# The samples' attention as a stream of its own in two weaves of a decoder step

## The chip, the cores and the metric

The kernel runs on one core of a Trainium2 chip, written in Python on a tile layer that allocates buffers from pools, sets all semaphores, and puts each engine's instructions into a fixed order when the program is built. The metric is the device time of one execution in microseconds, the median over runs. Engines are named as in the profile: PE (TensorE: matmuls), DVE (VectorE), ACT (ScalarE), POOL (GpSimd), SP (SyncE, which issues most transfers).

## The reference

One step of a two-layer decoder for a prompt of 1024 tokens and for eight samples of one token each, with the same weights (d = 1024, four heads of 128 in each attention, feed-forward width 2816). Layer 0 has a gated recurrence (HGRN2) beside attention into 256 memory tokens, layer 1 has stick-breaking attention beside the same kind of memory attention; a SwiGLU feed-forward follows each. What the change touches is the attention of the samples:

```
mem_attend(q, mk, mv):       s = q.k * dh**-0.5;  p = softmax(s);  o = p.v
stick_breaking(q, k, v, b):  z = q.k * dh**-0.5 + b
                             tail = sum over later keys of log_sigmoid(-z)
                             w = exp(log_sigmoid(z) + tail);  o = w.v
```

Each sample has 256 memory keys and values of its own in each layer, and in layer 1 two pages of 128 shared keys and values out of a paged pool (`cache_sb_k`, `cache_sb_v`, by `page_table`).

## The kernel before, in words

The prompt is worked in two groups of 512 tokens; group 1 also carries the eight samples as columns 512 to 519 of every activation tile. Activations stand with features on partitions. Every projection (`proj`, L256) streams 128x512 weights in: SP loads a raw piece of four 128x128 blocks (L245, pool of 5 buffers), ACT makes its rounded high half (L250), DVE its low half (L251), and PE runs three matmuls for each block: high weight with high and low input, low weight with high input (L264). Group 0 has one matmul of 512 columns each, group 1 two of 260. A projection's sum stands in one of two accumulators (`mm`), each emptied by ACT or DVE before it is used again: L281 and L474 in the gate and up half of the feed-forward, L403 in the down half.

The feed-forward (`ffn.part`, L464) is cut into five parts of 5, 5, 4, 4 and 4 blocks of the width; a part runs a gate and an up projection of 24 pieces for each block and then eight down projections of 15 or 12 pieces.

Stick-breaking for the prompt (`sb_prompt`, L1042) goes by head and by 128 keys: scores (L1058), bias and softplus on ACT and DVE, tail sums by matmuls with triangles (L1073) into a bank held for the whole head, weights by exp (L1081), value sums (L1085) into another bank held as long. So it holds two banks of the pool `s` (three banks), and the scores rotate through what is left. `mem_attn` (L621) goes by head and by pairs of 128 tokens: scores (L632), maximum (L637), exp (L643), normalised (L649), transposed (L656), value sums (L663).

For the samples, `sample_scores` (L671) copies each sample's query row out to all 128 partitions by a transfer from a scratch in memory (L689, on SP), multiplies the sample's keys with it (L690, DVE, 128x1024) and reduces by head (L691, DVE). `sample_pv` (L696) multiplies the values by the weights (L702, DVE), adds the two halves (L703, DVE), and sums over partitions by a matmul with a one-hot column block (L704, PE), all eight samples into one bank. Keys and values of the memory come by SP (L719), pages by an indirect transfer on POOL (L731); both go through the pool `c` of four buffers, which the prompt's memory attention uses for its own keys and values too.

The bank `ns` is a pool of one, used by `rstd_from` (L288) to sum squares over partitions for the norms, and for transposes in other stages.

All these are generators. `weave` (L222) takes streams with weights, and always steps the stream that is least far along by its weight; what it interleaves is the program's order, which the tile layer takes as the priority when it fixes each engine's order. The two weaves concerned are at L1172 (group 1's merge and memory attention of layer 0 beside group 0's feed-forward parts 2 and 3) and L1198 and L1199 (group 1's attention of layer 1 beside group 0's parts 0 to 3). After the first the last feed-forward part is drained, after the second the out projection (`o1.mm`) of group 1 begins, which reads what all attentions left in `xo`.

Of the kernel before, what the change touches and what calls it, by code (L numbers as in the profile page):

```python
# [22 lines left out]
def tile_decoder(  # L23
# [44 lines left out]
    def nm(s):  # L68
        uid[0] += 1
        return f"{s}_{uid[0]}"  # L70
# [4 lines left out]
    def B(dt=F32):  # L75
        return bpool.tile([P, 512], dt, tag="b", name=nm("b"))
# [4 lines left out]
    def NS():  # L81
        return nsp.tile([P, 512], F32, tag="ns", name=nm("ns"))
# [21 lines left out]
    def S():  # L104
        return smp.tile([P, 512], F32, tag="s", name=nm("s"))
# [107 lines left out]
    def drain(*gens):  # L213
        for g_ in gens:
            for _ in g_:
                pass

    def chain(*gens):
        for g_ in gens:
            yield from g_  # L220

    def weave(*streams):  # L222

        live = [[0, n, g_] for g_, n in streams]
        while live:
            cur = min(live, key=lambda e: e[0] / e[1])
            cur[0] += 1
            try:
                next(cur[2])
            except StopIteration:  # L230
                live.remove(cur)
# [38 lines left out]
    def split_to(dst, src):  # L270
        nc.scalar.copy(dst[0], src)  # L271
        nc.vector.tensor_sub(dst[1], src, dst[0].bitcast(F32))  # L272
# [421 lines left out]
            yield  # L694

    def sample_pv(pT, load, xo, k0):  # L696
        po = S()
        pv4 = pT.rearrange("p (k h b) -> p k h b", k=2, h=H)
        for b in range(NB):
            vt = load(b)  # L700
            v4 = vt.rearrange("p k (h d) -> p k h d", h=H)
            nc.vector.tensor_mul(v4, v4, pv4[:, :, :, b].unsqueeze(3).to_broadcast([P, 2, H, P]))  # L702
            nc.vector.tensor_add(vt[:, 0, :], vt[:, 0, :], vt[:, 1, :])  # L703
            nc.tensor.matmul(po[:NB, :], sel[:, b, :], vt[:, 0, :], start=(b == 0), stop=(b == NB - 1))  # L704
            yield
        ot = B()
        nc.vector.tensor_copy(ot[:NB, :], po[:NB, :])
        pr = S()
        for h in range(H):
            nc.tensor.transpose(pr[:, h * NB : (h + 1) * NB], ot[:NB, h * P : (h + 1) * P], ident[:NB, :NB])  # L710
        for h in range(H):
            d = xo[k0 + h]
            split_to((d[:, 0, G : G + NB], d[:, 1, G : G + NB]), pr[:, h * NB : (h + 1) * NB])
        yield
# [24 lines left out]
    def mem_attn_sample(l, qm, xo):  # L739
        HB = H * NB  # L740
        sc = small([P, 2 * HB], tag="sc", bufs=2)
        yield from sample_scores(qm, mem_loader(cache_mem_k, l), sc)
        pr = S()
        for blk in range(2):
            nc.tensor.transpose(pr[:HB, blk * P : (blk + 1) * P], sc[:, blk * HB : (blk + 1) * HB], ident)
        nmx = small([P, 2], tag="nmx")
        nc.vector.tensor_reduce(nmx[:HB, 0:1], pr[:HB, :NM], axis=AX.X, op=ALU.max, negate=True)
        sm = small([P, 2], tag="sme")
        pe = B()
        nc.scalar.activation(pe[:HB, :NM], pr[:HB, :NM], AF.Exp, bias=nmx[:HB, 0:1], accum_out=sm[:HB, 0:1])  # L750
        nc.vector.reciprocal(sm[:HB, 0:1], sm[:HB, 0:1])
        nc.vector.tensor_scalar(pe[:HB, :NM], pe[:HB, :NM], sm[:HB, 0:1], None, op0=ALU.mult)
        pb = S()
        for blk in range(2):
            nc.tensor.transpose(pb[:, blk * HB : (blk + 1) * HB], pe[:HB, blk * P : (blk + 1) * P], ident[:HB, :HB])
        pT = small([P, 2 * HB], tag="ss")
        nc.vector.tensor_copy(pT, pb[:, : 2 * HB])
        yield
        yield from sample_pv(pT, mem_loader(cache_mem_v, l), xo, H)
# [330 lines left out]
    def sb_sample(Qs, xo):  # L1090
        HB = H * NB
        zb = small([P, 2 * HB], tag="sc", bufs=2)
        yield from sample_scores(Qs, page_loader(cache_sb_k), zb)
        nc.vector.tensor_add(zb, zb, biass.rearrange("p k h b -> p (k h b)"))
        e = small([P, 2 * HB], tag="ss")
        softplus_sp(zb, e, 2 * HB)
        cu = S()
        nc.tensor.matmul(cu[:, 0:HB], trif, e[:, 0:HB], start=True, stop=False)
        nc.tensor.matmul(cu[:, 0:HB], ones, e[:, HB : 2 * HB], start=False, stop=True)
        nc.tensor.matmul(cu[:, HB : 2 * HB], trif, e[:, HB : 2 * HB], start=True, stop=True)  # L1100
        nc.vector.tensor_sub(zb, zb, cu[:, : 2 * HB])
        nc.scalar.activation(zb, zb, AF.Exp)
        yield
        yield from sample_pv(zb, page_loader(cache_sb_v), xo, 0)
# [57 lines left out]
    a1 = mixer_a(1, x1)  # L1162
# [5 lines left out]
    f0 = ffn(0, 0, o0.x)  # L1168
    weave((a1.core(), 22), (f0.part(0), 9))
    a1.open()  # L1170
    weave((a1.sample(), 6), (a1.gate(), 4), (f0.part(1), 9))
    weave((chain(a1.merge(), a1.mem_sample(), a1.mem()), 32), (chain(f0.part(2), f0.part(3)), 16))  # L1172
    drain(f0.part(4))
    xk0, xb0 = [], []
    o1 = out_proj(1, 0, M)
# [18 lines left out]
    b1 = mixer_b(1, xb1)  # L1194
    weave((b1.heads(), 8), (o0.finish(), 17))
    b1.open()
    f0 = ffn(0, 1, o0.x)
    weave((chain(b1.sb(), b1.mem()), 40), (chain(f0.part(0), f0.part(1)), 18))  # L1198
    weave((chain(b1.sb_sample(), b1.mem_sample()), 40), (chain(f0.part(2), f0.part(3)), 16))  # L1199
    o1 = out_proj(1, 1, A, True)  # L1200
    drain(o1.mm(b1.xo))
    weave((o1.finish(), 17), (f0.part(4), 8))
# [35 lines left out]
```

## Time and profile before

| | |
|---|---|
| median of 3 runs | 2554.57 us (2554.53 to 2558.19) |
| the profiled execution | 2554.25 us |
| its span in the profile | 2552.5 us |
| granted TensorE clock, mean | 0.995 |
| DMA queue "hardware_dynamic" | 286.92 MB, 37.3% of the engines' span |
| DMA queue "software_dynamic" | 8.39 MB, 1.1% |

The span leaves out 1.75 us around the program. Busy shares are unions of the instructions' times; matmuls are pipelined, and their ends are modelled. "PEclk" is the share of the full TensorE clock that was granted.

### The profile page before, as it was taken

The page shows a single profiled execution, that of the slowest core. Times are in us where ns is not written, and L with a number is a line of the kernel's source. Part 1 is how long each engine was busy: PE and PEld are TensorE (multiplying, and loading weights), DVE is VectorE, ACT ScalarE, POOL GpSimd, SP SyncE. Part 2 cuts the span into 40 slices and gives each one's busy share as a digit, 9 for nine tenths or more (in the row PEclk, how much of TensorE's full clock was granted, in tenths as well). Part 3 has the DMA queues.
Part 4 walks back from the last instruction along what each step waited for, and adds up shares of the span by engine and source line. Part 5 has one row for each costly group of instructions (what it writes and reads, how often), then busy time and mean ns, then how long its engine had stood idle before and what let it go on. Part 6 is the DMA issues. An engine that isn't in the chain of part 4 may idle for free.

```text
span 2552.5 us, 40535 instructions
## 1 busy us (share of the span) xinstructions
PE 2519.7 (99%) x15653; PEld 2194.2 (86%) x15653; DVE 1557.1 (61%) x2714; ACT 1183.8 (46%) x2187; POOL 41.3 (2%) x59
## 2 busy tenths in 40 slices
PE   8999999999999999999999999999999999999998
PEld 6888898878867888999999989767776798999998
DVE  6666566655675577555544577666678758444445
ACT  6346543243434445555433455566543245443334
POOL 1000000000000000000000000000021000000000
PEclk9999999999999999999999999999999999999999
DMA  6352242233552455322333445322156544323332
GB/s 185 109 162 71 73 151 76 66 112 117 172 179 83 132 156 172 102 85 60 99 92 93 127 151 181 110 85 71 53 175 212 154 125 128 108 87 101 94 92 67
DMA packets 457708, 297.91 MB, mean 117 GB/s; under 512 B 17573, under 2 KB 422642, under 8 KB 457514
## 3 DMA queue, kind: packets, MB, share of 16 engines
q1 hardware_dynamic: 454954, 286.92, 37.3%
q0 software_dynamic: 2560, 8.39, 1.1%
q8 instruction: 123, 2.02, 0.3%
q14 instruction: 71, 0.58, 0.1%
HBM read 265.44 MB, written 29.80 MB: 116 GB/s over the span
## 4 chain that ended last, share of the span: by engine, by line
issue 26%; PE 22%; POOL 1%; DVE 1%; DMA 0%; ACT 0%; POOLq 0%; DVEq 0%
PE mm L264 22%; POOL c L731 1%; PE s L704 0%; DVE c L690 0%; DMA c<-in_cache_sb_v,pidx 0%; DVE sc L691 0%; PE s L1135 0%; PE ns L293 0%; PE s L440 0%; DVE yT L542 0%; PE s L508 0%; DVE yT L539 0%; DVE ws L251 0%; POOLq L1234 0%; DVE t L474 0%
## 5 line engine op out<-in xcount | busy, mean ns | idle before, releaser
L264 PE MATMUL mm<-x,ws 128*128 128x260 f32 (+1 forms) x10080 | 1668.6, 323 | 7.8 <-DVE t L474 3.2
L264 PEld LDWEIGHTS mm<-x,ws 128*128 128x128 f32 x10080 | 1446.1, 189 | 170.0 <-issue 28.3
L250 ACT CAST ws<-w 128x512 fp32r<-128x512 f32 (+1 forms) x800 | 475.6, 595 | 910.4 <-PE mm L264 819.4
L251 DVE TENSOR_TENSOR ws<-w,ws 128x512 fp32r<-128x512 f32 (+1 forms) x800 | 522.4, 658 | 330.9 <-ACT ws L250 323.0
L264 PE MATMUL mm<-m,ws 128*128 128x260 f32 (+1 forms) x3168 | 543.0, 325 | 1.6 <-DVE t L474 0.9
L264 PEld LDWEIGHTS mm<-m,ws 128*128 128x128 f32 x3168 | 453.4, 188 | 60.3 <-issue 15.8
L403 DVE TENSOR_TENSOR r<-r,mm 128x520 f32<-128x520 f32 (+1 forms) x128 | 88.3, 690 | 89.0 <-PE mm L264 88.0
L281 DVE TENSOR_SCALAR t<-mm 128x512 f32<-128x512 f32 (+1 forms) x104 | 72.2, 694 | 108.2 <-PE mm L264 107.1
L474 DVE TENSOR_TENSOR t<-t,mm 128x512 f32<-128x512 f32 (+1 forms) x88 | 60.8, 691 | 116.1 <-PE mm L264 115.9
L285 DVE TENSOR_TENSOR t<-t,t 128x512 f32<-128x512 f32 (+1 forms) x88 | 61.2, 695 | 87.6 <-ACT t L284 87.5
L304 DVE TENSOR_TENSOR st<-st,n 128x512 f32<-128x512 f32 (+1 forms) x98 | 67.1, 691 | 6.9 <-ACT n L303 5.0
L272 DVE TENSOR_TENSOR m<-t,m 128x512 fp32r<-128x512 f32 (+1 forms) x88 | 61.0, 693 | 3.5 <-ACT m L271 1.6
L271 ACT CAST m<-t 128x512 fp32r<-128x512 f32 (+1 forms) x88 | 54.8, 623 | 15.7 <-DVE t L474 8.7
L282 ACT ACTIVATE t<-t 128x512 f32<-128x512 f32 (+1 forms) x88 | 55.8, 635 | 13.1 <-DVE t L281 5.7
L283 ACT ACTIVATE t<-t 128x512 f32<-128x512 f32 (+1 forms) x88 | 55.9, 635 | 2.6
L284 ACT ACTIVATE t<-t 128x512 f32<-128x512 f32 (+1 forms) x88 | 55.9, 635 | 2.3
L902 PEld LDWEIGHTS s<-a,a 128*128 128x128 f32 x448 | 53.4, 192 | 1.2
L902 PE MATMUL s<-a,a 128*128 128x64 f32 x448 | 53.1, 271 | 0.0
L731 POOL DMA_INDIRECT c<-in_cache_sb_k,pidx x16 | 16.6, 1037 | 1868.7 <-DVE r L403 1240.2
L1037 DVE SCALAR_TENSOR_TENSOR b<-b,b 128x512 f32<-128x512 f32 (+3 forms) x48 | 26.8, 558 | 29.6 <-ACT b L1036 29.2
L643 ACT ACTIVATE b<-s,nmx 128x256 f32<-128x256 f32 x64 | 29.8, 470 | 28.7 <-DVE nmx L637 28.7
L1085 PE MATMUL s<-b,a 128*128 128x512 f32 (+3 forms) x96 | 41.5, 514 | 0.3
(298 smaller groups left out, 1945.2 us busy)
## 6 DMA issues: line engine op xcount, KB each, us to landing
w<-in_w_gu SPq DMA_DIRECT2D x352, 256.0 KB
w<-in_w_down SPq DMA_DIRECT2D x160, 256.0 KB
w<-in_w_in_a SPq DMA_DIRECT2D x80, 256.0 KB
w<-in_w_o SPq DMA_DIRECT2D x64, 256.0 KB
w<-in_w_mem_kv SPq DMA_DIRECT2D x32, 256.0 KB
c<-in_cache_mem_k SPq DMA_DIRECT2D x16, 512.0 KB
c<-in_cache_mem_v SPq DMA_DIRECT2D x16, 512.0 KB
w<-in_w_kv SPq DMA_DIRECT2D x32, 256.0 KB
```

Source lines behind the costliest of these rows:

```text
L250: nc.scalar.copy(ws[:, 0, :n, :], raw[:, :n, :])
L251: nc.vector.tensor_sub(ws[:, 1, :n, :], raw[:, :n, :], ws[:, 0, :n, :].bitcast(F32))
L264: nc.tensor.matmul(ps[:, a, : PW[g]], wt, xt[k][:, xi, o : o + PW[g]], start=(k == 0 and wi == 0), stop=(k == nk - 1 and wi == 2),)
L272: nc.vector.tensor_sub(dst[1], src, dst[0].bitcast(F32))
L281: nc.vector.tensor_scalar(sv(x, g), pv(ps, g), -44.0, None, op0=ALU.max)
L283: nc.scalar.activation(d, d, AF.Ln, bias=1.0)
L284: nc.scalar.activation(d, d, AF.Exp, scale=-1.0)
L285: nc.vector.tensor_mul(d, d, x[:, :n])
L304: nc.vector.tensor_add(acc[:, :n], acc[:, :n], t[:, :n])
L403: nc.vector.tensor_add(dst, dst, pv(ps, g))
L474: nc.vector.tensor_mul(sv(sg, g), sv(sg, g), pv(pu, g))
L902: nc.tensor.matmul(plv[:, hh, c, :], K_[:, hh, cs], rhs, start=True, stop=True)
```

## The change

Three edits. The bank for the samples' value sums comes from `ns` in place of `s`. In the first layer's weave the samples' memory attention is no longer a piece of the chain between the merge and the prompt's memory attention, but a stream of its own beside both. In the second layer, two weaves one after the other (the prompt's attentions with feed-forward parts 0 and 1, then the samples' with parts 2 and 3) become one weave of three streams: the prompt's attentions, the samples' attentions, and the four parts. Lines behind the second weave move on by two.

```diff
     def sample_pv(pT, load, xo, k0):
-        po = S()
+        po = NS()
...
-    weave((chain(a1.merge(), a1.mem_sample(), a1.mem()), 32), (chain(f0.part(2), f0.part(3)), 16))
+    weave((chain(a1.merge(), a1.mem()), 12), (a1.mem_sample(), 20), (chain(f0.part(2), f0.part(3)), 16))
     drain(f0.part(4))
...
     f0 = ffn(0, 1, o0.x)
-    weave((chain(b1.sb(), b1.mem()), 40), (chain(f0.part(0), f0.part(1)), 18))
-    weave((chain(b1.sb_sample(), b1.mem_sample()), 40), (chain(f0.part(2), f0.part(3)), 16))
+    weave(
+        (chain(b1.sb(), b1.mem()), 40), (chain(b1.sb_sample(), b1.mem_sample()), 39),
+        (chain(f0.part(0), f0.part(1), f0.part(2), f0.part(3)), 34),
+    )
     o1 = out_proj(1, 1, A, True)
```

## The prediction

> **What bounds the kernel now.** I read the page first, then the busy time by stretch, then what TensorE waited for, and last the order in time around the longest of these waits.
>
> ```profile
> span 2552.5 us, 40535 instructions
> ...
> PE 2519.7 (99%) x15653; PEld 2194.2 (86%) x15653; DVE 1557.1 (61%) x2714; ACT 1183.8 (46%) x2187; POOL 41.3 (2%) x59
> ```
>
> TensorE carries the span, and the change neither adds nor takes away a matmul. Only what TensorE loses between matmuls can be won: idle time, and time at a lower clock. Which of it lies in the two changed stretches, the stretches show:
>
> ```profile
> core 0: us, PE busy (x) PEld busy (x) DVE busy (x) ACT busy (x) POOL busy (x), PEclk, DMA share, GB/s
> 1600.00:1870.00 270.00, 269.20 (x1131) 194.85 (x1130) 171.43 (x326) 163.57 (x328) 0.00 (x0) 1.00 0.27 79
> 1870.00:2030.00 160.00, 152.50 (x619) 110.39 (x618) 129.05 (x180) 51.30 (x95) 29.17 (x28) 0.97 0.65 200
> 675.00:750.00 75.00, 72.20 (x294) 52.02 (x293) 63.25 (x84) 24.55 (x41) 0.00 (x0) 1.00 0.67 203
> 1897.25:1904.07 6.82, 5.29 (x13) 4.13 (x13) 5.61 (x8) 0.56 (x1) 2.87 (x3) 0.50 0.79 243
> 1979.17:1982.58 3.41, 3.41 (x9) 2.64 (x9) 3.41 (x5) 0.00 (x0) 0.00 (x0) 0.50 0.87 240
> 559.22:562.63 3.41, 3.41 (x15) 1.61 (x12) 0.07 (x1) 0.00 (x0) 0.00 (x0) 0.50 1.11 327
> ```
>
> From 1600 to 1870 us the prompt's stick-breaking and memory attention run beside feed-forward parts 0 and 1: TensorE is idle for 270 - 269.20 = 0.8 us. From 1870 to 2030 us the samples' two attentions run beside parts 2 and 3: idle for 7.5 us, and VectorE is busy for 129.05 of 160 us (81%, against 63% before). The fourth and fifth rows are two pieces of that stretch in which the clock stood at half. The busy 5.29 + 3.41 us there would have taken half as long, so the half clock cost 4.35 us. From 675 to 750 us, in the first layer, the samples' attention costs 2.8 us of idle time at full clock.
>
> Who ended the idle time, from 1600 to 2030 us and then from 660 to 870 us:
>
> ```profile
> PE mm L264 <- DVE t L474: 3.2, 2, 1.8
> PE mm L264 <- DVE ws L251: 3.1, 2, 1.5
> PE s L704 <- DVE c L703: 1.2, 2, 1.0
> PE s L1073 <- ACT b L271: 0.4, 2, 0.3
> ```
>
> ```profile
> PE mm L264 <- DVE t L474: 0.9, 1, 0.9
> PE s L704 <- DVE c L703: 0.9, 1, 0.9
> ```
>
> It is VectorE nearly every time, and not with work of long duration: L474 empties a projection's bank, L251 makes the low half of a weight. They are late since they stand behind the samples' work in VectorE's queue. VectorE, then TensorE, around the first long wait:
>
> ```profile
> 1892.91 1.22 DVE L690 TENSOR_TENSOR c<-c,b 128x1024 f32<-128x1024 f32 x1 [1.60 <-issue]
> 1894.05 0.69 DVE L285 TENSOR_TENSOR t<-t,t 128x512 f32<-128x512 f32 x1
> 1894.65 1.21 DVE L691 TENSOR_REDUCE sc<-c 128x8 f32<-128x1024 f32 x1
> 1895.78 0.68 DVE L474 TENSOR_TENSOR t<-t,mm 128x512 f32<-128x512 f32 x1
> 1896.37 1.21 DVE L691 TENSOR_REDUCE sc<-c 128x8 f32<-128x1024 f32 x1
> 1897.50 0.68 DVE L272 TENSOR_TENSOR m<-t,m 128x512 fp32r<-128x512 f32 x1
> 1898.10 1.89 DVE L251 TENSOR_TENSOR ws<-w,ws 128x512 fp32r<-128x512 f32 x3
> ```
>
> ```profile
> 1896.60 0.70 PE L264 MATMUL mm<-x,ws 128*128 128x512 f32 x2 [1.81 <-DVE t L474]
> 1898.84 5.43 PE L264 MATMUL mm<-x,ws 128*128 128x512 f32 x12 [1.53 <-DVE ws L251]
> ...
> 1976.71 0.70 PE L264 MATMUL mm<-x,ws 128*128 128x512 f32 x2 [1.39 <-DVE t L474]
> 1978.95 4.38 PE L264 MATMUL mm<-x,ws 128*128 128x512 f32 x11 [1.54 <-DVE ws L251]
> ```
>
> Two samples' products and sums come in a row, the first held up for 1.60 us; L474 and the weights run after them, and TensorE stands for 1.81 and 1.53 us. From 1976 us the same happens again.
>
> **The change part by part.** *The later weave.* The samples' stream of 39 steps now lies beside all of the prompt's 40 and the 34 of the feed-forward. Instructions and transfers are the same in number; their order is not, on any engine. In the order in which the built programs' instructions stand, only two regions differ: this one, and the first layer's. On VectorE the samples' operations had stood in runs of up to four, with one other instruction or two between runs; now one product and one sum stand in each stretch of ten to sixteen instructions, and two or three together only where two values meet. On TensorE the prompt's chains keep their distance: as many matmuls of other work stand between a score and its tail sum as before.
>
> ```profile
> L691 DVE TENSOR_REDUCE sc<-c 128x8 f32<-128x1024 f32 x16 | 19.3, 1213 | 0.0
> L690 DVE TENSOR_TENSOR c<-c,b 128x1024 f32<-128x1024 f32 x16 | 19.1, 1221 | 1.6 <-issue 1.6
> L703 DVE TENSOR_TENSOR c<-c 128x512 f32<-128x512 f32 x16 | 10.7, 687 | 0.0
> L702 DVE TENSOR_TENSOR c<-c,sc 128x1024 f32<-128x1024 f32 x8 | 9.7, 1220 | 3.7 <-DMA c<-in_cache_sb_v,pidx 3.4 <-issue 0.3
> L702 DVE TENSOR_TENSOR c<-c,ss 128x1024 f32<-128x1024 f32 x8 | 9.6, 1221 | 0.3 <-DMA c<-in_cache_mem_v 0.2
> ```
>
> These 64 operations are 68.4 us of VectorE. All its work in the 430 us is 171.43 + 129.05 = 300.5 us: 70% everywhere in place of 63% and then 81%. A key step is 1.22 + 1.21 = 2.4 us, a value step 1.9 us. What covers one such step is a projection: TensorE has two accumulators, and works on the other while one is emptied. The shortest projections of these parts have 12 matmuls (15 in part 0), the gate and up ones 24:
>
> ```profile
> 1953.09 5.47 PE mm L264 x24
> ```
>
> So 0.228 us each, and covers of 2.7, 3.4 and 5.5 us, plus what the prompt's matmuls in between give. One step fits under each; two and a wait, as at 1892, do not. So I expect the 7.5 us of idle time and the 4.35 us of half clock that followed it to go: **-11.85 us**.
>
> What comes in its place: (1) The calm stretch's idle time, stretched: 0.8 us in 270 is 1.3 in 430, **+0.5**. (2) The query rows. Each of the 16 key steps needs one copied out to all partitions, and SP's queue has these copies among the weight loads, which wait for VectorE to free a raw buffer. From 1870 to 2030 us, and the copies with the first key step that used one:
>
> ```profile
> SPq L245 <- DVE ws L251: 71.0, 36, 13.3
> ```
>
> ```profile
> 1878.31 3.84 SPq L689 DMA_DIRECT2D b<-qd  x7
> ```
>
> ```profile
> 1882.10 1.23 DVE L690 TENSOR_TENSOR c<-c,b 128x1024 f32<-128x1024 f32 x1
> ```
>
> From issue to use are at most 3.8 us. In the new order five of the 16 copies have only 1.6 to 2.6 us of VectorE work between the release of the buffer ahead of them and their key step; at 70% load that is 2.3 to 3.7 us. VectorE then stands for 0.1 to 1.5 us, with an accumulator's evacuation behind it; two of the value loads stand alike. TensorE feels only what exceeds the cover. From nothing to seven times 1.5 = 10.5 us; I take **+1.5**, near the lower end, since seven copies in a row delayed VectorE by only 1.60 us above. (3) More turns between streams: the order has 956 changes into or out of L264 in place of 908, so 24 more interruptions. A matmul that waits for a signal took 0.05 us more than its like that seldom does:
>
> ```profile
> L1073 PE MATMUL s<-b,trir 128*128 128x512 f32 x40 | 18.1, 458 | 0.1
> L1073 PE MATMUL s<-b,cmpr 128*128 128x512 f32 x32 | 10.5, 408 | 0.0
> ```
>
> 24 x 0.05 = **+1.2**, from 0 to twice that (both sides of each may wait). (4) The end: the last prompt head's value product now stands inside the out projection's first piece, some 1.5 us of matmuls ahead of the piece that reads it. Its evacuation is two operations of 0.6 to 0.7 us, so nearly covered: 0, at most 1 us.
>
> *The first layer's weave.* The samples' memory attention starts at once beside the merge and the prompt's memory attention. Its 2.8 us of idle time could go. But in the new order the seventh and eighth query rows stand behind six weight loads, and both key steps, 4.9 us, come while TensorE runs projections of 12 matmuls with a cover of 2.7 us. I leave it at **0**, from -2.8 to +3.2 (a wait as at 1896, 1.81 + 1.53, over what goes).
>
> *The bank.* The value sums sit in the norm sums' bank for eight steps. Nobody else asks for it within either weave (the next norm sum comes after the out projection), so nothing waits: 0. It costs no less by itself, but the weave needs it: stick-breaking holds two of the three other banks, and a sum held in the third would leave none for the scores.
>
> Sum: -11.85 + 0.5 + 1.5 + 1.2 + 0 = -8.65 us. The profiled execution took 2554.25 us, so 2545.6; the median shown, 2554.57, lies 0.3 higher, and my forecast for it is **2545.9 us**. About 0.2% (5.1 us) is what a measurement of this kernel can tell from no change.
>
> **A rule against the trace.** The half clock began at 1897.25 us after idle pieces of at most 1.81 us. The Trainium skill ("TensorE: Matmul & The Clock Gate", Part 1: The HAM clock gate) has the clock fall after at least one idle window of about 3.4 us. No idle time here is so long, so by that rule these 4.35 us are not owed to the stalls, and the sum would be -4.3 us. The trace speaks against it in two places of three, where the half clock starts inside a stall or right after one; the third is the rival below.
>
> **The rivals.**
> - *The half clock is not the stalls'.* The last row of the stretches shows half clock from 559.22 us with TensorE busy for the whole 3.41 us, after thin matmuls (eight rows or columns). The samples' value sums, 128x8, are thin too. If it is they, the half clock stays, wherever they stand: 2545.9 + 4.35 = 2550.3 us. Against it: the same sums from 675 to 750 us left the clock at 1.00.
> - *The stalls only move.* VectorE's sum is unchanged, and some sample steps still meet an evacuation. If half of the 11.85 us stays: 2545.9 + 5.9 = 2551.8 us. For it: the late query rows. Against it: 63% load left 0.8 us idle in 270, and 70% is nearer to that than to 81%.
> - *Slower: query rows block VectorE.* It runs its queue in order; a row held behind weight loads that themselves wait for VectorE stops evacuations and weights together. One event of the kind at 1896 costs 1.81 + 1.53 us idle and 5.29 / 2 at half clock, 6.0 us. Two of them eat the gain up; with four, 2545.9 + 24 = 2570, with three 2563.9 us, the time I give it. It decides once VectorE stands for more than a cover (2.7 to 5.5 us) at a key step. Against it: the longest of VectorE's waits there now is 1.60 us.
>
> **How the numbers follow.** Forecast 0.65, stalls move 0.17, half clock stays 0.06, slower 0.12. The forecast's own range is 2539 (nothing comes in place of the 11.85 us and the first layer's 2.8 goes too) to 2549. For 8 in 10 I reach over the two middle rivals: **2539 to 2553 us**. Faster by over 0.2% (below 2549.5): the forecast and a little of the next, 0.68. Within 0.2%: 0.20. Slower: 0.12.
>
> **What would show it.** Right: in the stretch of some 420 us from the first stick-breaking score to the out projection TensorE idles for 1 to 5 us, the clock stays at 1.00, VectorE's load is level at 70%, and all else keeps its length. Wrong: half-clock pieces at the samples' sums with no idle time (the first rival); waits for L251, L474 or L403 summing to 5 us or more behind L690 (the second and third); a longer stretch without idle time would mean that the turns between streams are dearer than 0.05 us.

## The result, and the profile after

The changed kernel takes 2551.05 us (median of 22 runs, 2548.63 to 2553.59), the kernel before, beside it on the same chips, 2555.13 us (22 runs). The ratio is 0.9984 with a 95% interval of 0.9978 to 0.9991: 4.1 us or 0.16% faster, where 8.65 us were forecast. The profiled execution took 2551.36 us; the head of its page:

```profile
span 2549.6 us, 40536 instructions
...
PE 2518.9 (99%) x15653; PEld 2193.2 (86%) x15653; DVE 1557.2 (61%) x2714; ACT 1186.6 (47%) x2187; POOL 43.8 (2%) x59
```

The engines' work is what it was, and 2.9 us of the span are gone. To see where, I cut the span of each trace at matmuls that every version has: the last one of the samples' recurrence in layer 0 (L853), the first transpose of the first key and value projection (L1014), the first transpose of the samples' keys at the end of the second one (L1027), the next norm sum (L293, after the second weave and its out projection), and the last matmul. Each piece is read from one profiled execution. us:

| kernel | start | first layer's piece | between | second layer's piece | remainder |
|---|---|---|---|---|---|
| before | 609.51 | 323.78 | 620.58 | 528.12 | 464.34 |
| after | 608.66 | 319.93 | 620.40 | 529.94 | 464.35 |

The first layer's weave, entered at nothing in the forecast, gave 3.85 us. The second layer's, for which it was made, gave nothing: 1.8 us longer, which is within the scatter (with the old second weave this piece took 528.1 to 530.2 us in three kernels below). (The expectations below quote these two pieces between slightly different marks, as 311.3 to 307.2 and 474.5 to 476.3; the differences are the same within 0.3 us. All pieces in this part go by the table's marks.)

The busy time by stretch, after: the second weave as a whole, three parts of it, the half clock in it, and the first layer's row of before's list.

```profile
core 0: us, PE busy (x) PEld busy (x) DVE busy (x) ACT busy (x) POOL busy (x), PEclk, DMA share, GB/s
1600.00:2030.00 430.00, 421.22 (x1730) 302.67 (x1729) 300.87 (x506) 216.51 (x421) 27.86 (x24) 0.99 0.41 123
1600.00:1700.00 100.00, 99.03 (x425) 74.45 (x423) 69.12 (x113) 54.29 (x104) 14.45 (x14) 1.00 0.46 139
1700.00:1800.00 100.00, 94.16 (x359) 64.00 (x359) 66.86 (x116) 50.03 (x93) 13.41 (x10) 0.97 0.41 120
1800.00:2030.00 230.00, 228.03 (x950) 164.21 (x949) 164.88 (x280) 112.19 (x225) 0.00 (x0) 1.00 0.40 116
1708.30:1715.13 6.83, 5.51 (x15) 4.47 (x16) 4.79 (x10) 1.44 (x4) 2.24 (x2) 0.50 0.34 83
675.00:750.00 75.00, 75.00 (x325) 57.93 (x325) 51.72 (x81) 30.82 (x61) 0.00 (x0) 1.00 0.47 133
```

VectorE's load is level, 300.87 of 430 us or 70%, as forecast. But TensorE still idles for 8.78 us (8.3 before), 5.84 of them between 1700 and 1800 us, and the half clock there costs 5.51 / 2 = 2.75 us. The last row has no idle time left where before had 2.8 us. Who ended TensorE's idle time from 1600 to 2030 us (total, times, longest):

```profile
PE s L1073 <- DVE b L272: 5.3, 2, 3.7
PE s L1085 <- DVE b L1040: 1.5, 2, 1.3
PE s L1073 <- ACT b L271: 0.9, 2, 0.6
PE s L1073 <- DVE b L1078: 0.2, 1, 0.2
```

Every row of before's list is gone: no L264 waits for L474 or L251 any more. In their place the prompt's own tail sums and value sums (L1073, L1085) wait for VectorE. And VectorE, in the same stretch, waits for transfers:

```profile
DVE c L690 <- DMA b<-qd: 10.7, 9, 4.0
...
DVE c L702 <- DMA c<-in_cache_sb_v,pidx: 3.8, 3, 2.7
...
DVE c L702 <- DMA c<-in_cache_mem_v: 2.1, 3, 1.5
```

The longest such wait in order of time, first in SP's issues, then on VectorE, then on TensorE:

```profile
1700.47 0.55 SPq L689 DMA_DIRECT2D b<-qd  x1
```

```profile
1703.68 0.29 DVE L1040 TENSOR_TENSOR b<-b,sm 128x128 f32<-128x128 f32 x1
1708.00 1.23 DVE L690 TENSOR_TENSOR c<-c,b 128x1024 f32<-128x1024 f32 x1 [4.02 <-DMA b<-qd]
1709.14 0.42 DVE L272 TENSOR_TENSOR b<-b,b 128x256 fp32r<-128x256 f32 x1
```

```profile
1704.86 1.10 PE L264 MATMUL mm<-m,ws 128*128 128x512 f32 x4
1709.62 0.58 PE L1073 MATMUL s<-b,trir 128*128 128x256 f32 x1 [3.66 <-DVE b L272]
1710.00 2.77 PE L264 MATMUL mm<-m,ws 128*128 128x512 f32 x6
```

The query row is issued at 1700.47 and used at 1708.00, 7.5 us later; 1700 to 1708 us is full of other transfers (254 GB/s there, against 123 over the weave). VectorE runs its queue in order and stands at L690 for 4.02 us. Behind it is L272, the low half of a softplus piece, and TensorE, in order too, has L1073 next, which reads it. A second accumulator is no help: the projection's matmuls stand behind L1073.

### The profile page after: what moved, and what is told of

Same layout as the page of the kernel before. It is cut to its first block, busy times and chain, and to the rows that moved or that the text cites. A ratio compares the mean times of both kernels' runs of the same rounds, so it can differ in the third digit from the quotient of the medians.

```text
span 2549.6 us, 40536 instructions
## 1 busy us (share of the span) xinstructions
PE 2518.9 (99%) x15653; PEld 2193.2 (86%) x15653; DVE 1557.2 (61%) x2714; ACT 1186.6 (47%) x2187; POOL 43.8 (2%) x59
## 5 line engine op out<-in xcount | busy, mean ns | idle before, releaser
L264 PE MATMUL mm<-x,ws 128*128 128x260 f32 (+1 forms) x10080 | 1668.4, 323 | 1.4 <-ACT x L355 1.3
L264 PEld LDWEIGHTS mm<-x,ws 128*128 128x128 f32 x10080 | 1443.1, 188 | 166.3 <-issue 29.2
L251 DVE TENSOR_TENSOR ws<-w,ws 128x512 fp32r<-128x512 f32 (+1 forms) x800 | 523.5, 657 | 324.0 <-ACT ws L250 314.6
L264 PE MATMUL mm<-m,ws 128*128 128x260 f32 (+1 forms) x3168 | 544.4, 326 | 0.1
L264 PEld LDWEIGHTS mm<-m,ws 128*128 128x128 f32 x3168 | 455.1, 189 | 53.9 <-issue 7.1
L403 DVE TENSOR_TENSOR r<-r,mm 128x520 f32<-128x520 f32 (+1 forms) x128 | 88.3, 690 | 99.2 <-PE mm L264 97.7
L474 DVE TENSOR_TENSOR t<-t,mm 128x512 f32<-128x512 f32 (+1 forms) x88 | 60.8, 691 | 117.2 <-PE mm L264 117.2
L272 DVE TENSOR_TENSOR m<-t,m 128x512 fp32r<-128x512 f32 (+1 forms) x88 | 61.0, 694 | 3.7 <-ACT m L271 1.6
L1073 PE MATMUL s<-b,trir 128*128 128x512 f32 (+3 forms) x96 | 38.0, 397 | 7.6 <-DVE b L272 5.3
L1085 PE MATMUL s<-b,a 128*128 128x512 f32 (+3 forms) x96 | 41.6, 515 | 1.9 <-DVE b L1040 1.5
```

Source lines behind the costliest of these rows:

```text
L251: nc.vector.tensor_sub(ws[:, 1, :n, :], raw[:, :n, :], ws[:, 0, :n, :].bitcast(F32))
L264: nc.tensor.matmul(ps[:, a, : PW[g]], wt, xt[k][:, xi, o : o + PW[g]], start=(k == 0 and wi == 0), stop=(k == nk - 1 and wi == 2),)
L403: nc.vector.tensor_add(dst, dst, pv(ps, g))
L474: nc.vector.tensor_mul(sv(sg, g), sv(sg, g), pv(pu, g))
```

## The experiments

The first theory: late query rows block VectorE, and that eats the second weave's gain up. The rivals: VectorE's load itself, the bank, SP's queue, or other transfers. "Before" in each result is the kernel before, beside it on the same chip.

**One part of the change at a time.** `e_first` takes the second weave's edit back, `e_second` the first one's, `e_bank` both:

```
e_first, e_bank:
-    weave((chain(b1.sb(), b1.mem()), 40), (chain(b1.sb_sample(), ...), 39), (chain(f0.part(0), ...), 34))
+    weave((chain(b1.sb(), b1.mem()), 40), (chain(f0.part(0), f0.part(1)), 18))
+    weave((chain(b1.sb_sample(), b1.mem_sample()), 40), (chain(f0.part(2), f0.part(3)), 16))
e_second, e_bank:
-    weave((chain(a1.merge(), a1.mem()), 12), (a1.mem_sample(), 20), (chain(f0.part(2), f0.part(3)), 16))
+    weave((chain(a1.merge(), a1.mem_sample(), a1.mem()), 32), (chain(f0.part(2), f0.part(3)), 16))
```

> Only the first layer's weave (and the bank); the second layer as before. In the traces, the piece from the samples' recurrence to the first key and value projection took 311.3 us before and 307.2 after, and the piece with the second layer's weave 474.5 and 476.3. Theory: all of the gain is the first layer's, so this kernel gains 4 us by itself, 0.998 of before, as much as both edits together or more. Rival, as the prediction had it: the second weave carries the gain, and this one is 0 (1.000).

> Only the second layer's weave (and the bank); the first layer as before. Theory: nothing won, since what left the projections' waits came back as waits of the prompt's attention: -1 to +2 us, 1.000 of before. Rival, the prediction: -8.65 us, 0.9966.

> Only the bank of the samples' value sums; both weaves as before. Both theories: nothing, 0 +- 1 us, as the sum has a bank to itself either way. If the bank frees the third score bank for earlier work, up to -1 us.

Measured, against 2553.87 us before (11 runs each): `e_first` 2551.16 us, 0.9991 (0.9982 to 1.0); `e_second` 2554.06, 0.9999 (0.999 to 1.0008); `e_bank` 2553.83, 0.9997 (0.9988 to 1.0006). The first layer's piece is 319.73 us in `e_first`, 323.53 and 323.45 in the two others. The interval of `e_first` just reaches 1, so the times alone don't decide; the pieces do: the gain is the first layer's, the second weave's edit is worth nothing as it stands, and the bank costs nothing that shows.

**No query rows from memory.** `e_noq` leaves out layer 1's query rows and multiplies the sample keys by a tile that is on the chip anyway (in short):

```
-            qb = B()
-            nc.sync.dma_start(qb, qd[b].partition_broadcast(P))
+            qb = row        # layer 1: carry.rearrange("p h k -> p (h k)")
```

> The whole change, but in the second layer the samples' keys are multiplied by a tile that lies ready in the buffers (the recurrent state), not by the query row copied out by a transfer: 16 transfers of 256 KB less, and no wait for them; the samples' outputs are then not theirs. Theory: VectorE's 10.7 us of waits for query rows are what holds up the prompt's chain and idles TensorE, so its idle time in the second weave falls from 8.8 us to 3 us or less and no half clock is left there: 5 to 9 us faster than the change as it is (0.995 to 0.997 of before). Rival: the prompt's chain is held up by VectorE's load of 70% and the one bank left for scores, and the time stays at 0.998.

Measured: 2548.23 us (11 runs), 0.9976 (0.9967 to 0.9985). The second layer's piece falls to 522.94 us, 7.0 less than after, with 4.3 us of idle time from 1600 to 2030 us and no half clock, but the first layer's grows from 319.93 to 325.12. Without the query the products depend on nothing in layer 1, and some run early in the first layer, where they block an accumulator once. TensorE from 700 to 900 us:

```profile
PE mm L264 <- DVE t L474: 3.5, 1, 3.5
```

So this run doesn't settle it: work that left the second weave makes it shorter too. `e_cols` keeps the dependency, and takes the query from the tile of its columns, which hold its features by partition (so the products are not the ones wanted, but as many and as large):

```
+                k4 = kt.rearrange("p k (h d) -> p k h d", h=H)
+                q4 = qc.rearrange("p (h b) -> p h b", h=H)[:, :, b].unsqueeze(1).unsqueeze(3)
+                nc.vector.tensor_mul(k4, k4, q4.to_broadcast([P, 2, H, P]))
```

> The whole change, but in the second layer the samples' keys are multiplied by columns that stand in the buffers from the weave's start on (the query's features by partition) in place of the copied row: no 256 KB copies there, the same count and size of VectorE operations, and they cannot start before the weave; the samples' outputs are then not theirs. It mends the run before it, where the products had run ahead into the first layer: there the second layer's piece was 7.0 us shorter than with the change (529.94 to 522.94 us) and the first layer's 5.2 us longer. Theory: the query rows' waits are what idles TensorE, so the second layer's piece is 5 to 7 us shorter than with the change, the first layer's the same: 0.996 of before. Rival (load of VectorE, one bank for scores): the piece stays near 530 us, 0.998.

Measured: 2549.96 us (11 runs), 0.9989 (0.998 to 0.9998) against 2553.4; the second layer's piece 529.96 us, as in after. **The first theory falls**: without a query row the time is the same. TensorE and VectorE in the same stretch of `e_cols` (L1078 is L1073 of after, L691 the key product, L707 the value product):

```profile
PE s L1078 <- ACT b L271: 4.7, 1, 4.7
```

```profile
DVE c L707 <- DMA c<-in_cache_sb_v,pidx: 5.1, 4, 2.6
...
DVE c L691 <- DMA c<-in_cache_sb_k,pidx: 4.4, 1, 4.4
...
DVE c L691 <- DMA c<-in_cache_mem_k: 1.8, 2, 1.0
...
DVE c L707 <- DMA c<-in_cache_mem_v: 0.5, 2, 0.3
```

The stall has moved to the next transfer: one page of keys holds VectorE until 1608.25 us, for 4.4 us. Behind it on VectorE stands the softplus piece (L1039 there) that ScalarE and then L1078 go by, and TensorE stands for 4.7 us, until 1613.31 us. The new theory: it is not this copy but any load whose product comes to VectorE's head before the data.

**Another queue for the rows.** `e_qact` issues the same copies from ScalarE's queue, so that they don't stand behind weight loads on SP:

```
-            nc.sync.dma_start(qb, qd[b].partition_broadcast(P))
+            nc.scalar.dma_start(qb, qd[b].partition_broadcast(P))
```

> The whole change, with the query rows' copies issued from ACT's queue, not SP's, in both layers: they no longer stand behind weight loads, though their place in time and the transfers beside them are the same. If the rows are late since SP issues them late: waits for rows fall under 3 us, 5 us won, 0.996 of before. If they are late since the transfer itself takes long beside page gathers, weights and keys (issue at 1700.5 us, first use at 1708.0): waits stay near 10 us, and the time at 0.998, or worse, as ACT spends 16 issues more.

Measured: 2550.99 us (11 runs), 0.9991 (0.9982 to 1.0); second layer's piece 528.34. VectorE's waits:

```profile
DVE c L690 <- DMA b<-qd: 8.1, 8, 2.5
...
DVE c L702 <- DMA c<-in_cache_sb_v,pidx: 3.5, 3, 2.5
```

8.1 us in place of 10.7: SP's queue is at most a quarter of it, and the time is the same.

**Products held back until their data can be there.** `e_hold` copies each query row one step ahead, and puts layer 1's key products behind one of two VectorE operations of the other streams, whichever stands last before them in the program: the product in a feed-forward block (L474 of after) or the subtraction from a tail sum (L1078). So they can't be placed much earlier than the weave has them:

```
+    def behind(on):
+        return tc.issue_after(mark[0].ins) if on else nullcontext()
-                nc.vector.tensor_mul(sv(sg, g), sv(sg, g), pv(pu, g))
+                mark[0] = nc.vector.tensor_mul(sv(sg, g), sv(sg, g), pv(pu, g))
...
-                nc.vector.tensor_sub(zb[:, :w], zb[:, :w], rr[:, c0:])
+                mark[0] = nc.vector.tensor_sub(zb[:, :w], zb[:, :w], rr[:, c0:])
...
+            if b + 1 < NB or not late:
+                rows.append(row(b + late))
+            with behind(late):
+                nc.vector.tensor_mul(kt, kt, qb.unsqueeze(1).to_broadcast([P, 2, 512]))
```

`e_holdv` does the same with the value steps:

```
+        ahead = [load(0)] if late else []
...
+            if b + 1 < NB or not late:
+                ahead.append(load(b + late))
+            vt = ahead.pop(0)
+            with behind(late):
+                nc.vector.tensor_mul(v4, v4, pv4[:, :, :, b].unsqueeze(3).to_broadcast([P, 2, H, P]))
```

and `e_vonly` holds the value steps alone.

> The whole change, and in the second layer each query row is copied out one step ahead, while its product is put behind the last VectorE operation of the other two streams that stands before it in the program: 7 to 14 us of VectorE work between the release ahead of the copy and the product, where there were 2 to 7. The same work, the same outputs. Theory: the waits for query rows go (10.7 us to under 2), and with them 5 to 7 us of the second layer's piece: 0.996 of before. Rival one (load): 0.998. Rival two: putting products later fills the end of the weave and moves the stall there, 0.998 or above.

> As the run before, and the value steps likewise: loaded one step ahead, their product put behind the other streams. VectorE waited 2.7 us for one value page with the change. Theory: another 0 to 2 us: 0.995 to 0.996 of before. Rival two (the end of the weave) is stronger here: the last value sum stands later, and the out projection may wait for it, up to 3 us lost.

> Of the run with both kinds of step put behind the other streams (0.9949 of before, 2540.3 us, TensorE idle for 0.5 us of 430) only the value steps; the query rows come as in the change. Theory, as mended by the runs so far: any transfer that VectorE waits for in its queue can stop TensorE, and with one kind taken away the other still does, so the two gains do not add: rows alone gave 2.4 us of the second layer's piece, this one gives 2 to 5 of the 11.7 that both give, 0.996 to 0.998 of before. Rival: the value pages were the whole cause, and this run equals the one with both, 0.995.

`e_hold`: 2549.52 us (11 runs), 0.9987 (0.9978 to 0.9996); second layer's piece 527.55, 2.4 us less than after where 5 to 7 were expected. The rows' waits are gone, those for values have grown (L718; TensorE's L1089 is L1073 of after):

```profile
DVE c L718 <- DMA c<-in_cache_sb_v,pidx: 9.3, 4, 5.0
```

```profile
PE s L1089 <- ACT b L276: 4.3, 1, 4.3
PE s L1089 <- DVE b L277: 2.1, 2, 1.6
```

`e_holdv`: **2540.32 us** (2539.57 to 2542.41, 5 runs) against 2553.4, 0.9949 (0.9936 to 0.9963); second layer's piece 518.21, another 9.3 us less where 0 to 2 were expected. Its stretches, and all that VectorE still waits for transfers:

```profile
1600.00:1870.00 270.00, 269.65 (x1109) 193.05 (x1108) 184.89 (x318) 145.13 (x274) 24.69 (x24) 1.00 0.43 130
1870.00:2030.00 160.00, 159.87 (x710) 117.44 (x709) 116.03 (x196) 75.17 (x155) 0.00 (x0) 1.00 0.38 115
1600.00:2030.00 430.00, 429.52 (x1818) 310.49 (x1817) 300.92 (x513) 220.30 (x429) 24.69 (x24) 1.00 0.41 124
```

```profile
DVE c L722 <- DMA c<-in_cache_mem_v: 0.5, 1, 0.5
```

The same instructions, VectorE with the same 301 us, and TensorE idle for 0.48 us in 430, at full clock. `e_vonly`: 2547.02 us (10 runs), 0.9974 (0.9964 to 0.9983) against 2554.58; piece 522.39, 7.6 us less than after where 2 to 5 were expected, with the rows' waits still there:

```profile
DVE c L706 <- DMA b<-qd: 6.8, 8, 2.7
```

So each half of the hold takes part of it away, and only both take all. From 1600 to 2030 us TensorE's idle time goes with VectorE's waits for transfers, of either kind: 8.78 us idle for 16.6 us of waits in after, 7.20 for 11.1 in `e_hold`, 4.24 for 6.8 in `e_vonly`, 0.48 for 0.5 in `e_holdv`. `e_noq`, which holds nothing back, lies between them as well (4.26 for 6.9). In the weave of three streams the cause is these waits. Which part of the hold takes them away, the load one step ahead or the place behind other work, no run separates. Why the order has the products so early is not shown either: that the tile layer puts an instruction in place once its own estimate has the data landed is only argued.

**Is the third stream needed?** `e_two` is `e_holdv` with the second weave's edit taken back, so that the samples' work stands in the last 160 us only. `e_all` is `e_holdv` with the first layer's steps held as well (`late=True` in both layers).

> Both kinds of step put behind the other streams, and the first layer's new weave, but in the second layer the two weaves one after the other, as before the change. Tells whether the weave of three streams is needed. Theory: yes. VectorE is busy for 81% of the samples' stretch there and its waits came from its own queue, more than from transfers: the second layer's piece stays at 525 us or more (518.2 with three streams, 528.1 before), 0.998 of before. Rival: the late steps alone are the gain, and the piece falls to 518 to 520 us, 0.995.

> Both kinds of step put behind the other streams, in the first layer too. The first layer's piece has no idle time left with the change (319.9 us), so theory: nothing more, 0.995 of before, the piece at 319 to 320 us. Rival: later steps there push the samples' last value sum toward the end, 1 to 3 us lost.

`e_two`: 2543.79 us (5 runs) against 2554.58, 0.9959 (0.9945 to 0.9972); second layer's piece 520.03. The last 160 us of its weaves, the half clock in them, and the one stall on TensorE (L269 is L264 of after, L408 is L403):

```profile
1870.00:2030.00 160.00, 157.88 (x692) 117.14 (x692) 130.20 (x184) 54.07 (x98) 34.41 (x26) 0.99 0.68 204
1933.99:1937.40 3.41, 3.41 (x8) 2.23 (x8) 1.68 (x2) 0.00 (x0) 2.31 (x2) 0.50 0.72 186
```

```profile
1932.51 0.94 PE L269 MATMUL mm<-m,ws 128*128 128x512 f32 x3 [2.03 <-DVE r L408]
```

VectorE is busy for 130.20 of 160 us, 81%, as before, and TensorE idles for 2.12 us in place of 7.5. So the load of 81% was not what held TensorE up, and the theory of this run (525 us or more) falls. But here it was not the waits for transfers either. `e_first` has the same two weaves without the hold; TensorE's waits there, then VectorE's waits for transfers in `e_first` and in `e_two`, from 1600 to 2030 us:

```profile
PE mm L264 <- DVE t L474: 4.6, 2, 2.7
PE mm L264 <- DVE ws L251: 3.1, 2, 1.5
```

```profile
DVE c L702 <- DMA c<-in_cache_sb_v,pidx: 2.6, 3, 1.5
DVE c L690 <- DMA b<-qd: 1.8, 2, 1.6
DVE c L702 <- DMA c<-in_cache_mem_v: 0.5, 2, 0.2
```

```profile
DVE c L722 <- DMA c<-in_cache_sb_v,pidx: 3.1, 2, 1.7
DVE c L722 <- DMA c<-in_cache_mem_v: 1.1, 2, 0.6
DVE c L706 <- DMA b<-qd: 1.0, 1, 1.0
```

VectorE waits as long (5.2 us against 4.9), and the waits for L474 and L251 are gone. So with two streams the gain is one of order: the hold puts the sample products behind L474, the operation that TensorE had waited for. The link from order to gain is read from these rows; no run isolates it. `e_holdv` and `e_two` overlap in their intervals; that three streams are better than two once the products are held is not settled.

`e_all`: 2543.71 us (5 runs), 0.9957 (0.9943 to 0.997). The first layer's piece is 321.95 us, 2.1 more than in `e_holdv` (319.81):

```profile
PE s L661 <- DVE b L654: 2.0, 2, 1.7
```

There TensorE waits for the prompt's memory attention in place. By the pieces the change as it is was better in the first layer than holding; the intervals of the whole times overlap.

**The second layer's piece, taken apart.** Over windows of 2 us I summed TensorE's idle time and what the half clock cost (busy time by one less the granted clock); what is left of the piece is matmul time at full clock (the clock is rounded in each window, so 2.72 stands here for the 2.75 above). us:

| kernel | streams | piece | idle | half clock | left |
|---|---|---|---|---|---|
| before | 2 | 528.12 | 8.58 | 4.25 | 515.3 |
| e_bank | 2 | 530.23 | 9.23 | 5.82 | 515.2 |
| e_first | 2 | 529.13 | 9.71 | 4.41 | 515.0 |
| e_two | 2 | 520.03 | 3.20 | 1.70 | 515.1 |
| after | 3 | 529.94 | 9.27 | 2.72 | 517.9 |
| e_second | 3 | 529.07 | 9.05 | 1.70 | 518.3 |
| e_noq | 3 | 522.94 | 4.75 | 0 | 518.2 |
| e_cols | 3 | 529.96 | 9.58 | 3.05 | 517.3 |
| e_qact | 3 | 528.34 | 8.65 | 1.69 | 518.0 |
| e_hold | 3 | 527.55 | 7.52 | 2.79 | 517.2 |
| e_vonly | 3 | 522.39 | 4.51 | 0 | 517.9 |
| e_holdv | 3 | 518.21 | 0.76 | 0 | 517.5 |
| e_all | 3 | 518.36 | 0.85 | 0 | 517.5 |

The last column falls into two groups: 515.0 to 515.3 with two streams at a time, 517.2 to 518.3 with three. The third stream costs 1.9 to 3.3 us of matmul time by itself, whatever else is changed; in the pairs that differ in this weave alone (`e_first` and after, `e_bank` and `e_second`, `e_two` and `e_holdv`) it is 2.4 to 3.1 us.

## Why the prediction was right in its direction and wrong in its size

The time lies inside the stated 2539 to 2553 us, and the direction was right, but by luck: the second layer's piece, for which -8.65 us stood, came out no shorter, and the gain came from the first layer's, for which 0 stood. Of the signs named for being right only the level load of 70% came; TensorE idled for 8.78 us, not for 1 to 5, and there was half clock. The signs named for being wrong were half clock with no idle time, waits for L251, L474 or L403, and a longer stretch with no idle time; the waits that came, at L1073 and L1085, are none of these.

- **The -11.85 us (idle 7.5, half clock 4.35).** The waits that it names did go: not one wait of L264 for L474 or L251 is left. One key or value step per stretch of other work does fit under a projection, as forecast, and VectorE's load is level at 70%. That the idle time and the half clock can be won nearly whole is shown by `e_holdv` (0.76 us left of 12.8 in the piece).
- **Term (2), the late query rows: the step that failed.** The prediction saw that rows would come late and took +1.5 us, since "TensorE feels only what exceeds the cover". It measured the cover by the projections' accumulators. What stood behind the waiting L690 was the prompt's stick-breaking chain, and the matmul that needed it was next on TensorE: 3.66 us of a 4.02 us wait came through. It forecast five late copies, each holding VectorE for 0.1 to 1.5 us; nine did, for up to 4.02 us and 10.7 us in all. The row above took 7.5 us from issue to use. "At most 3.8" was read from the first of seven copies alone, and the 1.60 us taken as the price of such copies is a wait for which the profile names no transfer ("issue"). And the term named query rows and "two of the value loads" only; `e_cols` and `e_hold` show that pages and memory values take their place as soon as the rows are no longer waited for. With the half clock that they set off, these waits cost up to 9.27 + 2.72 = 12.0 us in the piece, for 12.8 lost in before: term (2), entered at 1.5 and at most 10.5, ate nearly all of the first term.
- **Term (3), the turns between streams.** Too small: +1.2 was taken, 0 to 2.4 allowed; the table gives 2.7 for after (517.95 against 515.29). By line it is not the projections, whose matmuls take 400.5 us of the piece in before and 400.4 in after, but the attentions' matmuls between them (114.8 and 117.6 us). That it is the turns isn't isolated, and their number doesn't set it: the piece has 331 changes into or out of L264 in before, 363 in `e_hold` (517.2 us left), 373 in `e_second` (518.3) and 385 in `e_holdv` (517.5).
- **Term (1)** is not to be told apart from term (2) here. **Term (4)**, the end: TensorE idles for 0.2 us between 2030 and 2105 us in after and not at all in before, within the "0, at most 1 us".
- **The first layer's weave, entered at 0.** It gave 3.85 us, a little beyond the -2.8 of its range. From 610 to 935 us TensorE idled for 3.01 us before and for 0.03 after; the feared wait under projections of 12 matmuls did not come. The other 0.9 us is a shorter matmul time that I can't place.
- **The bank**: `e_bank` 0.9997, nothing, as said.
- **The rivals.** "The stalls only move" gives 2551.8 us, and 2551.05 was measured: its mechanism, stalls that move, is what happened in the second weave, though to the prompt's chain and not to an evacuation; that the figure is so near is luck, since the first layer's gain is in the sum as well. "Slower: query rows block VectorE" named the right place and the wrong price: one event of the kind, not three. "The half clock is not the stalls'" falls for this weave: `e_holdv` has the same thin value sums and no half clock in it.
- **The clock rule.** The half clock of after began at 1708.30 us, when its stall had lasted 2.34 us (since 1705.96); in before and in `e_two` it followed stalls of 1.81 and 2.03 us. The Trainium skill ("TensorE: Matmul & The Clock Gate", Part 1: The HAM clock gate) wants an idle window of some 3.4 us. None of these three agrees with it; `e_cols` does, where the half clock began 4.24 us into a stall of 4.65. What the traces show is a grid: the half clock of before began at 559.22, 1897.25 and 1979.17 us, which lie 392 and 24 times 3.413 us apart, and within each other trace the starts lie on such a grid too. In the two changed weaves the 3.41 us ahead of a start held 1.8 us of idle time or more in every kernel that had one (1.81 in before, 1.94 in `e_two`, 2.34 in after, 3.41 in `e_cols`). The most that such a step held with no half clock behind it was 1.63 us: in `e_vonly` the grid cuts a stall of 2.31 us in two.

## What to carry to other kernels

In a queue that runs in order, an instruction that waits for a transfer stops all that stands behind it; so ask of each added wait which chain stands there, and whether its reader can be passed, before an accumulator is counted as cover. When work is spread over a longer stretch, spread its loads too: issue each one step ahead, and place its consumer no earlier than that step, in the order and not just in the program's text (both together did it here; neither was tried alone). Place it also behind what the bottleneck engine waits for: in the old weave that, more than the data, seems to have been the gain. And weaving one stream more costs busy time of its own (here 2 to 3 us in 528), so see first whether better placing within the old weave gives the same.

## What the runs showed of the hardware that was not expected

- The half clock came in pieces of 3.41 us or twice that. Stalls of 1.81 us (before), 2.03 us (`e_two`) and 3.66 us (after) were followed by it, one of 2.31 us (`e_vonly`) was not.
- It also came with no idle time at all. Near 605 us, in the samples' recurrence of layer 0, after matmuls with eight rows or columns (L850, L853), after shows

```profile
605.80:609.20 3.40, 3.40 (x16) 1.87 (x14) 0.08 (x1) 0.00 (x0) 0.00 (x0) 0.50 0.91 287
```

  with TensorE busy throughout. Every version has such a piece between 558 and 612 us; the value sums in the second weave, 128x8, never had one in `e_holdv`.
- A copy of one query row to all partitions was used 7.5 us after its issue in after (1700 to 1708 us, 254 GB/s), with VectorE waiting for it. At the eight other waits for a row there it was 3.4 to 5.1 us. In before the first of seven copies in a row was used 3.8 us after its issue, with no wait (1878 to 1882 us, 191 GB/s). Whether the other traffic makes the difference isn't shown.
